# A decoder layer on one core: the first norm's last squares and root under the query product, keys and values leave PSUM unscaled, sums on VectorE, first loads in another order

## The chip, the core and the metric

The kernel runs on one core of a Trainium2 chip. The core has five engines that run side by side, each with its own in-order instruction stream: TensorE (PE, matrix products; PEld is its weight load), VectorE (DVE), ScalarE (ACT), GpSimd (POOL) and SyncE (SP, which here only issues transfers). Transfers between the chip's main memory and the on-chip memory SBUF are issued by SP, ACT or POOL and carried out by 16 DMA engines. TensorE writes to PSUM, from where DVE or ACT take the results. The metric is the device time of one execution in microseconds (us), and of several runs the median.

## The reference

One layer of a decoder for 320 tokens (256 of a prompt, 8 x 8 samples), D = 2048, all in float32. The beginning matters here:

```python
def rms_norm(x, g):
    xf = x.astype(jnp.float32)
    y = xf * lax.rsqrt(jnp.mean(xf * xf, axis=-1, keepdims=True) + EPS)
    return (y * g.astype(jnp.float32)).astype(x.dtype)
...
    xn = rms_norm(x, g_mix)
    z = xn @ w_in          # [B | C | h | q | k | v | gate_conv | gate_attn]
    u = c_gate * h_conv
    conv_out, conv_state = short_conv(u, conv_prev, w_conv)
    y_conv = (b_gate * conv_out) @ w_conv_out
    ...                    # banded attention of 16 query heads over 4 key/value heads
    merged = jax.nn.sigmoid(gate_c) * y_conv + jax.nn.sigmoid(gate_a) * y_attn
    h = x + merged @ w_o
    hn = rms_norm(h, g_ffn)
    h = h + (jax.nn.silu(hn @ w_gate) * (hn @ w_up)) @ w_down
```

The outputs are the final norm of h, and the new keys, values and convolution state. The scaled keys and values are outputs themselves.

## The kernel before

**Products.** Activations lie with features on the 128 partitions and the 320 tokens along the free side: x is 16 chunks of 128 x 320. A float32 product is made of three: each weight tile is split into a rounded part `whi` (an ACT copy, line 94) and a residual `wlo` (a DVE subtraction, line 95), and each x chunk into `xh_t` (ACT, line 244) and `xl_t` (DVE, line 245); TensorE adds whi.xh, whi.xl and wlo.xh. In the order of `passes` the wlo matmuls run a few steps behind the whi matmuls of the same tile. The raw weights have four buffers (`wraw`), the parts three each (`whi`, `wlo`): a load waits until DVE has read the raw buffer, a split until TensorE has read the part buffer.

**The norm is applied late.** x goes into the products unscaled (times g_mix only); the scale 1/root of each token, `rb`, is multiplied onto the results. `rb` needs the sum of squares of all 16 chunks (`xacc`): a square per chunk (even chunks on ACT, odd on DVE, lines 318 and 320), added up by POOL (line 322), one matmul with `ones` that sums over partitions (`prb`, line 350), and `rstd_of`/`inv_root` (lines 177 to 189): scale, ACT's root, DVE's reciprocal, three DVE products that refine it. `rbq` and `rbsq` follow from `rb`.

**The stages.** First the keys and values: `kv_product` makes all four 128-column groups of k and v at once, in nine weight tiles (two of one x chunk, seven of two; lines 265 to 293), into all four `acc` banks of PSUM. Ahead of it TensorE runs seven matmuls on a constant (`wm`, line 238). Inside it, at one place of each tile, `x_prep` makes the parts of the next two x chunks, and `tick()` lets `start_rest` issue the next piece of side work: squares and sums, the small loads on POOL's queue, the position-bias table (`pe_`, line 337, `e_sb`, `e_scr`, `bias_s`) and at last the root. After the product, kT and vT are the PSUM results times `rb` (lines 358 and 360). Then four query products (`in_pair`, named q, 16 weight tiles in all) with `kv_work` as side work: `kv_natural` transposes vT and kT on TensorE, `keys_twice` makes the keys' parts. The first query tile's split is tied behind the root by `first`. After q come the products C, H, B with the attention as side work, the gates, the output products and the feed-forward part; they are not touched.

**First loads.** x comes in eight blocks (`XB`, in chunks of 128 x 320: 1, 1, 2, 2, 2, 2, 2, 4). SP issues x blocks 0, 1, 2, then by turns a key/value weight tile and an x block; ACT issues the first two weight tiles. `small_loads` (POOL) waits for x chunk 3.

**Order.** A scheduler lays out each engine's stream from data dependences and the `after(...)` marks; pools of buffers (`bufs=`) add the waits.

Of the kernel before, what the change touches and what calls it, by code (L numbers as in the profile page):

```python
# [8 lines left out]
F32 = mybir.dt.float32  # L9
F32R = mybir.dt.float32r  # L10
AF = mybir.ActivationFunctionType
ALU = mybir.AluOpType
# [5 lines left out]
T = TP + NB * TS  # L18
DC = 1024
NH, NKV, HD, GRP = 16, 4, 64, 4  # L20
DKV = NKV * HD
WIN = 128
NBK = 32
FF = 5632
EPS = 1e-6
NEG = -1.0e30
P = 128
KC = D // P
CW = 256
KT = 4  # L30
O_B, O_C, O_H, O_Q = 0, DC, 2 * DC, 3 * DC
O_GC = O_Q + NH * HD
O_GA = O_GC + D
EL = 384
# [7 lines left out]
def hybrid_layer(ctx: ExitStack, tc: tile.TileContext, a: dict, o: list):  # L42
    nc = tc.nc
# [16 lines left out]
    def ps_aux(name):  # L60
        return aux.tile([P, 512], F32, tag="aux", name=name)
# [3 lines left out]
    def u(s):  # L65
        uid[0] += 1
        return f"{s}_{uid[0]}"

    def after(*marks):

        es = ExitStack()
        for m in marks:
            es.enter_context(tc.issue_after(m.ins))
        return es
# [3 lines left out]
    def tmp(tag, name):  # L78
        return wk.tile([P, UL], F32, tag=tag, name=u(name))
# [7 lines left out]
        lo = wp.tile([P, KT, CW], F32R, tag="wlo", name=u("wlo"), bufs=3)  # L87
        return hi, lo

    first = []  # L90

    def split_to(hi, lo, src):
        with after(*first):
            last["hi"] = nc.scalar.activation(hi, src, AF.Copy)  # L94
            last["lo"] = nc.vector.tensor_sub(lo, src, hi.bitcast(F32))  # L95

    def load_cols(w, k0, n, c0, behind=()):
        raw = raw_tile()
# [7 lines left out]
    side_work = [None]  # L106
# [67 lines left out]
    def rstd_of(ss, shape, name, pool, out=None):  # L174

        v = pool.tile(shape, F32, tag=f"rs_v{shape[1]}", name=u(name))
        nc.vector.tensor_scalar(v, ss, 1.0 / D, EPS, op0=ALU.mult, op1=ALU.add)
        return inv_root(v, shape, name, pool, out)
# [28 lines left out]
    def in_pair(c0, name, **kw):  # L207
        return product(lambda k0, n: load_cols(w_in, k0, n, c0), KC, xh, xl, name, **kw)
# [4 lines left out]
    kT = zz.tile([P, 2, T], F32, name="kT")  # L213
    vT = zz.tile([P, 2, T], F32, name="vT")
    vn = [zz.tile([P, DKV], F32, name=f"vn{t}") for t in range(3)]


    sp = ExitStack()
# [15 lines left out]
    )  # L234

    wm = ps_aux("wm")
    for _ in range(7):
        nc.tensor.matmul(wm, busy[:, :P], busy, start=True, stop=True)

    def x_prep(kc):  # L240
        if kc == 0:
# [10 lines left out]

    def load_kv(k0, n):
        raw = wp.tile([P, KT // 2, CK], F32, tag="wraw", name=u("wraw"), bufs=4)
        (nc.scalar if k0 < 2 else nc.sync).dma_start(raw[:, :n, :], w_kv[0, :, k0:k0 + n, :])
        hi = wp.tile([P, KT // 2, CK], F32R, tag="whi", name=u("whi"), bufs=3)
        lo = wp.tile([P, KT // 2, CK], F32R, tag="wlo", name=u("wlo"), bufs=3)
        with after(*mark[k0]):
            split_to(hi[:, :n, :], lo[:, :n, :], raw[:, :n, :])
        return hi, lo  # L260

    def kv_product(tiles, x_after):

        ps = [ps_acc(u("kv")) for _ in range(4)]
        k0 = 0
        x_prep(0)
        for i, n in enumerate(tiles):
            hi, lo = load_kv(k0, n)
            if i == 0:
                x_prep(1)  # L270
            for b in x_after.get(i, ()):
                x_load(b)
            order = [(k, c) for k in range(n) for c in range(4)]
            if k0 + n == KC:
                order.sort(key=lambda kc: kc[1])
            seq = passes(order, k0 + n == KC)
            if i == 0:
                seq.sort(key=lambda kcm: kcm[2])
            for k, c, m in seq:
                kc = k0 + k  # L280
                if k0 and (k, c, m) == (0, 1 if n == 1 or k0 + 2 * n == KC else 3, 0) and k0 + n < KC:
                    x_prep(k0 + n)
                    x_prep(k0 + n + 1)
                    tick()
                w, x = ((hi, xh), (hi, xl), (lo, xh))[m]
                last["mm"] = nc.tensor.matmul(  # L286
                    ps[c][:, :T], w[:, k, c * P:(c + 1) * P], x(kc),
                    start=(kc == 0 and m == 0), stop=(kc == KC - 1 and m == 2),
                )
            k0 += n  # L290
            if i == 0:
                tick()
        return ps

    rel = st.tile([NBK, NH], F32, name="rel")
    oh = st.tile([NBK, WIN], F32, name="oh")
    sk = a["sinks"]
    gate = st.tile([P, 1], F32, name="gate")

# [8 lines left out]
            nc.gpsimd.dma_start(st_sb, a["state_t"])  # L308
            nc.gpsimd.dma_start(blk, a["c_block"])

    xacc = st.tile([P, T], F32, name="xacc")

    def squares(*chunks):

        for k in chunks:
            t = xacc if k == 0 else st.tile([P, T], F32, tag="sq", name=u("sq"), bufs=4)
            if k % 2 == 0:
                nc.scalar.activation(t, hT[:, k, :], AF.Square)
            else:
                nc.vector.tensor_mul(t, hT[:, k, :], hT[:, k, :])  # L320
            if k:
                nc.gpsimd.tensor_tensor(xacc, xacc, t, op=ALU.add)

    def start_rest():
        squares(0)
        yield
        small_loads()
        squares(1)
        yield
        squares(2, 3, 4)  # L330
        yield
        squares(5, 6, 7)
        yield
        squares(8, 9, 10, 11)
        nc.vector.tensor_scalar(nsink, sink_bc, -1.0, None, op0=ALU.mult)
        pe_ = ps_aux("pe_")
        nc.tensor.matmul(pe_[:NH, :WIN], rel, oh, start=True, stop=True)
        e_sb = st.tile([NH, EL], F32, name="e_sb")
        nc.vector.memset(e_sb, NEG)
        nc.vector.tensor_copy(e_sb[:, WIN - 1:2 * WIN - 1], pe_[:NH, :WIN])  # L340
        nc.gpsimd.dma_start(e_scr, e_sb)
        yield
        squares(12, 13, 14, 15)
        yield
        nc.gpsimd.dma_start(
            bias_s, bass.AP(e_scr.tensor, e_scr.offset + WIN - TS, [[EL, NH], [1, TS], [1, WIN + TS]])
        )
        yield
        prb = ps_aux("prb")
        nc.tensor.matmul(prb[:, :T], ones, xacc, start=True, stop=True)  # L350
        rstd_of(prb[:, :T], [P, T], "r1", st, out=rb)

    side_work[0] = start_rest()
    ps_kv = kv_product([1, 1] + [2] * 7, {0: (2,), 2: (3,), 3: (4,), 4: (5, 6), 5: (7,)})
    for _ in side_work[0]:
        pass
    for c in range(2):
        nc.vector.tensor_mul(kT[:, c, :], ps_kv[c][:, :T], rb)
    for c in range(2):
        nc.vector.tensor_mul(vT[:, c, :], ps_kv[2 + c][:, :T], rb)  # L360
    nc.vector.tensor_scalar(rbq, rb, HD ** -0.5, None, op0=ALU.mult)
    nc.vector.tensor_mul(rbsq, rb, rb)
    sp.close()
    first += [last["root"], last["inv"]]

    yp = ExitStack()
    yy = yp.enter_context(tc.tile_pool(name="yy", bufs=1))
# [279 lines left out]
            yield  # L647

    def kv_work():
        for t in range(3):  # L650
            kv_natural(t)
            yield
        yield from keys_twice()
# [23 lines left out]
    side_work[0] = kv_work()  # L677
    for j in range(2):
        for gp in range(2):
            ps = in_pair(O_Q + (j * 2 + gp) * CW, "q", loaded=first.clear)  # L680
            pending.append(lambda j=j, gp=gp, ps=ps: q_out(j, gp, ps))
    side_work[0] = attention()

# [433 lines left out]
```

## Time and profile before

| what | value |
|---|---|
| median of 3 runs | 1690.41 us (1690.31 to 1691.01) |
| the profiled execution, its own time | 1690.07 us |
| its span, from first to last instruction | 1688.0 us |
| TensorE busy, share of the span | 1672.2 us, 99% |
| DVE / ACT / POOL busy | 902.4 / 645.9 / 97.3 us |
| mean granted TensorE clock | 0.997 |
| first matmul of keys and values, of the queries | 5.11 us, 44.53 us |

How to read the rows that follow. In a timeline a row has the start and the length in us, the engine, the line of the kernel, the operation, what it writes and reads (buffer numbers left out), the shape, and how many such instructions in a row were merged (x4); in brackets the idle time of the engine before it and what ended that. Rows of one engine can overlap a little, as a following instruction enters before the one ahead has left. In a row of waits: the total, the number of waits, the longest. In a table of stages: first the stretch (us from the span's start) and its length, then for each engine the busy time and in brackets the number of instructions, then the granted TensorE clock (1.00 is full), the busy share of the DMA engines and GB/s. A row of a load ends with the time from issue to landing.

### The profile page before, as it was taken

What the parts mean: (1) busy time and instruction counts of PE and PEld (TensorE: products, weight loads), DVE (VectorE), ACT (ScalarE), POOL (GpSimd) and SP (SyncE); (2) the same over time, 40 slices, a digit from 0 to 9 for tenths busy, and PEclk for the clock granted to TensorE, in tenths of its full rate; (3) what the DMA queues carried; (4) which work ended last, traced back from release to release, by engine and by line L of the source; (5) the groups of instructions that cost most, each with busy time, mean ns of one, the idle gap of its engine ahead of it and who ended that gap; (6) DMA issues with size and microseconds to landing.
All of it is one profiled execution on the core that took longest, in us unless ns stands there. A gap on an engine that the chain in (4) does not pass through costs nothing.

```text
span 1688.0 us, 26587 instructions
## 1 busy us (share of the span) xinstructions
PE 1672.2 (99%) x11016; PEld 1624.3 (96%) x11016; DVE 902.4 (53%) x1351; ACT 645.9 (38%) x898; POOL 97.3 (6%) x135
## 2 busy tenths in 40 slices
PE   8999999999999999999999999999999999999998
PEld 7999999999999999999999999998888999999887
DVE  8679564444444445546555555553444455555556
ACT  5455443333333333334333333333333333334344
POOL 6001311000000002320000000000000000000000
PEclk9999999999999999999999999999999999999999
DMA  6554545544454444444444444445555444444543
GB/s 229 162 156 143 183 134 164 176 149 149 150 150 150 150 150 150 150 149 148 150 150 150 150 150 150 150 150 151 150 151 150 150 150 150 150 150 150 174 145 105
DMA packets 76336, 258.13 MB, mean 153 GB/s; under 512 B 8440, under 2 KB 15016, under 8 KB 76088
## 3 DMA queue, kind: packets, MB, share of 16 engines
q1 hardware_dynamic: 73960, 250.01, 47.5%
q0 software_dynamic: 1968, 5.90, 1.2%
q8 instruction: 86, 1.41, 0.3%
q10 hardware_dynamic: 288, 0.52, 0.1%
q14 instruction: 34, 0.28, 0.0%
HBM read 253.29 MB, written 5.08 MB: 153 GB/s over the span
## 4 chain that ended last, share of the span: by engine, by line
PE 98%; POOL 1%; DVE 1%; DMA 0%; issue 0%; SPq 0%; ACT 0%; DVEq 0%; POOLq 0%
PE fg L141 18%; PE fu L141 18%; PE dn L837 9%; PE ga L141 7%; PE wo L141 7%; PE gc L141 7%; PE dn L845 6%; PE H L141 3%; PE C L141 3%; PE B L141 3%; PE q L141 3%; PE ya L141 3%; PE yc L141 3%; PE dl L841 2%; PE dr L992 1%; PE kv L286 1%
## 5 line engine op out<-in xcount | busy, mean ns | idle before, releaser
L95 DVE TENSOR_TENSOR wlo<-wraw,whi 128x1024 fp32r<-128x1024 f32 (+1 forms) x464 | 568.7, 1226 | 642.4 <-ACT whi L94 633.8
L94 ACT ACTIVATE whi<-wraw 128x1024 fp32r<-128x1024 f32 (+1 forms) x464 | 490.5, 1059 | 811.3 <-PE dn L837 179.9
L837 PE MATMUL dn<-a_t,whi 128*128 128x512 f32 x672 | 231.0, 396 | 0.0
L141 PE MATMUL fu<-hh_t,whi 128*128 128x320 f32 x704 | 212.6, 310 | 0.0
L141 PE MATMUL fg<-hh_t,whi 128*128 128x320 f32 x704 | 212.4, 309 | 0.0
L141 PE MATMUL fu<-hl_t,whi 128*128 128x320 f32 x704 | 212.3, 309 | 0.0
L141 PE MATMUL fg<-hl_t,whi 128*128 128x320 f32 x704 | 212.3, 309 | 0.0
L141 PE MATMUL fg<-hh_t,wlo 128*128 128x320 f32 x704 | 164.0, 309 | 0.0
L141 PE MATMUL fu<-hh_t,wlo 128*128 128x320 f32 x704 | 164.0, 309 | 0.0
L845 PE MATMUL dn<-a_t,wlo 128*128 128x320 f32 x672 | 159.5, 309 | 0.0
L837 PEld LDWEIGHTS dn<-a_t,whi 128*128 128x128 f32 x672 | 125.1, 188 | 24.6 <-issue 0.5
L141 PEld LDWEIGHTS fu<-hl_t,whi 128*128 128x128 f32 x704 | 132.2, 188 | 0.1
L141 PEld LDWEIGHTS fu<-hh_t,whi 128*128 128x128 f32 x704 | 132.1, 188 | 0.1
L141 PEld LDWEIGHTS fg<-hl_t,whi 128*128 128x128 f32 x704 | 132.2, 188 | 0.0
L141 PEld LDWEIGHTS fg<-hh_t,whi 128*128 128x128 f32 x704 | 132.1, 188 | 0.0
L845 PEld LDWEIGHTS dn<-a_t,wlo 128*128 128x128 f32 x672 | 118.0, 188 | 11.7
L141 PEld LDWEIGHTS fu<-hh_t,wlo 128*128 128x128 f32 x704 | 118.5, 188 | 0.0
L141 PEld LDWEIGHTS fg<-hh_t,wlo 128*128 128x128 f32 x704 | 118.5, 188 | 0.0
L141 PE MATMUL wo<-m_h,whi 128*128 128x320 f32 x256 | 77.2, 309 | 0.0
L141 PE MATMUL ga<-xh_t,whi 128*128 128x320 f32 x256 | 77.1, 308 | 0.0
L141 PE MATMUL ga<-xl_t,whi 128*128 128x320 f32 x256 | 77.1, 308 | 0.0
L141 PE MATMUL gc<-xh_t,whi 128*128 128x320 f32 x256 | 77.1, 308 | 0.0
(278 smaller groups left out, 2759.2 us busy)
## 6 DMA issues: line engine op xcount, KB each, us to landing
wraw<-in_w_in_dram SPq DMA_DIRECT2D x128, 512.0 KB, 3.8
wraw<-in_w_gate_dram SPq DMA_DIRECT2D x88, 512.0 KB, 3.8
wraw<-in_w_up_dram SPq DMA_DIRECT2D x88, 512.0 KB, 3.8
wraw<-in_w_down_dram SPq DMA_DIRECT2D x88, 512.0 KB, 3.6
wraw<-in_w_o_dram SPq DMA_DIRECT2D x32, 512.0 KB, 3.7
wraw<-in_w_conv_out_dram SPq DMA_DIRECT2D x16, 512.0 KB, 3.7
wraw<-in_w_attn_out_dram SPq DMA_DIRECT2D x16, 512.0 KB, 3.7
wraw<-in_w_kv_dram SPq DMA_DIRECT2D x7, 512.0 KB, 6.9
```

Source lines behind the costliest of these rows:

```text
L94: last["hi"] = nc.scalar.activation(hi, src, AF.Copy)
L95: last["lo"] = nc.vector.tensor_sub(lo, src, hi.bitcast(F32))
L141: last["mm"] = nc.tensor.matmul(ps[c][:, :T], w[:, k, c * P:(c + 1) * P], x(kc), start=(kc == 0 and i == 0), stop=(kc == nk - 1 and i == 2),)
L286: last["mm"] = nc.tensor.matmul(ps[c][:, :T], w[:, k, c * P:(c + 1) * P], x(kc), start=(kc == 0 and m == 0), stop=(kc == KC - 1 and m == 2),)
L837: nc.tensor.matmul(ps[c], parts[k][0][:, cs], a_t[:, k, 0:512], start=k == 0, stop=False)
L841: nc.tensor.matmul(low[:, :w], a_t[:, k, 512:], parts[k][0], start=k == 0, stop=k == nf - 1)
L845: last["mm"] = nc.tensor.matmul(ps[c][:, :T], parts[k][1][:, cs], a_t[:, k, 0:T], start=False, stop=k == nf - 1)
L992: last["mm"] = nc.tensor.matmul(ps[:, :CW], x, w, start=(t == 2 and k == 0 and m == 0), stop=(k == nf - 1 and m == len(ms) - 1),)
```

## The change

- POOL no longer adds squares. All squares are made on ACT, into buffers of the work pool (`tmp`, two for each of four tags), and all sums on DVE.
- The squares of chunks 12 to 15, the sum over partitions, the root, `rbq`, `rbsq` and the position-bias table move out of `start_rest` into `first_norm`, side work at the head of `kv_work`, under the query products. The two matmul groups `pe_` and `prb` stand behind the second query tile.
- ACT copies keys and values from PSUM unscaled; `first_norm` multiplies them by `rb` in SBUF later, and the transposes of `kv_natural` come three ticks later.
- The tie `first` of the query splits to the root is gone.
- The second weight tile is issued by SP, behind x block 1 and ahead of x block 2; x block 2 was issued ahead of the weight tiles. The first weight tile is copied by ACT in two halves. The warm-up is six matmuls of 512 columns and three of 128.
- `x_prep` and `tick` stand a little later in most tiles.

```diff
@@ -87,12 +87,9 @@
         lo = wp.tile([P, KT, CW], F32R, tag="wlo", name=u("wlo"), bufs=3)
         return hi, lo
 
-    first = []
-
     def split_to(hi, lo, src):
-        with after(*first):
-            last["hi"] = nc.scalar.activation(hi, src, AF.Copy)
-            last["lo"] = nc.vector.tensor_sub(lo, src, hi.bitcast(F32))
+        last["hi"] = nc.scalar.activation(hi, src, AF.Copy)
+        last["lo"] = nc.vector.tensor_sub(lo, src, hi.bitcast(F32))
 
     def load_cols(w, k0, n, c0, behind=()):
         raw = raw_tile()
@@ -213,6 +210,10 @@
     kT = zz.tile([P, 2, T], F32, name="kT")
     vT = zz.tile([P, 2, T], F32, name="vT")
     vn = [zz.tile([P, DKV], F32, name=f"vn{t}") for t in range(3)]
+    xacc = zz.tile([P, T], F32, name="xacc")
+    rel = zz.tile([NBK, NH], F32, name="rel")
+    oh = zz.tile([NBK, WIN], F32, name="oh")
+    e_sb = zz.tile([NH, EL], F32, name="e_sb")
 
 
     sp = ExitStack()
@@ -234,8 +235,8 @@
     )
 
     wm = ps_aux("wm")
-    for _ in range(7):
-        nc.tensor.matmul(wm, busy[:, :P], busy, start=True, stop=True)
+    for n in [512] * 6 + [P] * 3:
+        nc.tensor.matmul(wm[:, :n], busy[:, :P], busy[:, :n], start=True, stop=True)
 
     def x_prep(kc):
         if kc == 0:
@@ -252,11 +253,16 @@
 
     def load_kv(k0, n):
         raw = wp.tile([P, KT // 2, CK], F32, tag="wraw", name=u("wraw"), bufs=4)
-        (nc.scalar if k0 < 2 else nc.sync).dma_start(raw[:, :n, :], w_kv[0, :, k0:k0 + n, :])
+        (nc.scalar if k0 == 0 else nc.sync).dma_start(raw[:, :n, :], w_kv[0, :, k0:k0 + n, :])
         hi = wp.tile([P, KT // 2, CK], F32R, tag="whi", name=u("whi"), bufs=3)
         lo = wp.tile([P, KT // 2, CK], F32R, tag="wlo", name=u("wlo"), bufs=3)
         with after(*mark[k0]):
-            split_to(hi[:, :n, :], lo[:, :n, :], raw[:, :n, :])
+            if k0 == 0:
+                nc.scalar.activation(hi[:, 0, :CW], raw[:, 0, :CW], AF.Copy)
+                last["hi"] = nc.scalar.activation(hi[:, 0, CW:], raw[:, 0, CW:], AF.Copy)
+                last["lo"] = nc.vector.tensor_sub(lo[:, 0, :], raw[:, 0, :], hi[:, 0, :].bitcast(F32))
+            else:
+                split_to(hi[:, :n, :], lo[:, :n, :], raw[:, :n, :])
         return hi, lo
 
     def kv_product(tiles, x_after):
@@ -278,7 +284,7 @@
                 seq.sort(key=lambda kcm: kcm[2])
             for k, c, m in seq:
                 kc = k0 + k
-                if k0 and (k, c, m) == (0, 1 if n == 1 or k0 + 2 * n == KC else 3, 0) and k0 + n < KC:
+                if k0 and (k, c, m) == (0, 3 if n > 1 else 1, 0) and k0 + n < KC:
                     x_prep(k0 + n)
                     x_prep(k0 + n + 1)
                     tick()
@@ -292,8 +298,6 @@
                 tick()
         return ps
 
-    rel = st.tile([NBK, NH], F32, name="rel")
-    oh = st.tile([NBK, WIN], F32, name="oh")
     sk = a["sinks"]
     gate = st.tile([P, 1], F32, name="gate")
 
@@ -308,60 +312,61 @@
             nc.gpsimd.dma_start(st_sb, a["state_t"])
             nc.gpsimd.dma_start(blk, a["c_block"])
 
-    xacc = st.tile([P, T], F32, name="xacc")
-
     def squares(*chunks):
 
         for k in chunks:
-            t = xacc if k == 0 else st.tile([P, T], F32, tag="sq", name=u("sq"), bufs=4)
-            if k % 2 == 0:
-                nc.scalar.activation(t, hT[:, k, :], AF.Square)
-            else:
-                nc.vector.tensor_mul(t, hT[:, k, :], hT[:, k, :])
+            t = tmp("t" + "abcd"[k % 4], "sq")[:, :T] if k else xacc
+            nc.scalar.activation(t, hT[:, k, :], AF.Square)
             if k:
-                nc.gpsimd.tensor_tensor(xacc, xacc, t, op=ALU.add)
+                nc.vector.tensor_add(xacc, xacc, t)
 
     def start_rest():
         squares(0)
         yield
         small_loads()
         squares(1)
-        yield
-        squares(2, 3, 4)
-        yield
-        squares(5, 6, 7)
-        yield
-        squares(8, 9, 10, 11)
+        for k in range(2, 12, 2):
+            yield
+            squares(k, k + 1)
+
+    side_work[0] = start_rest()
+    ps_kv = kv_product([1, 1] + [2] * 7, {1: (2,), 2: (3,), 3: (4,), 4: (5, 6), 5: (7,)})
+    for _ in side_work[0]:
+        pass
+    for c in range(2):
+        nc.scalar.activation(kT[:, c, :], ps_kv[c][:, :T], AF.Copy)
+    for c in range(2):
+        nc.scalar.activation(vT[:, c, :], ps_kv[2 + c][:, :T], AF.Copy)
+    sp.close()
+
+    class spare:
+
+        @staticmethod
+        def tile(shape, dtype, tag, name):
+            return tmp({"v": "tb", "s": "tc", "r": "td"}[tag[3]], name)[:, :shape[1]]
+
+    def first_norm():
+
+        squares(12, 13, 14, 15)
         nc.vector.tensor_scalar(nsink, sink_bc, -1.0, None, op0=ALU.mult)
-        pe_ = ps_aux("pe_")
+        nc.vector.memset(e_sb, NEG)
+        yield
+        prb, pe_ = ps_aux("prb"), ps_aux("pe_")
         nc.tensor.matmul(pe_[:NH, :WIN], rel, oh, start=True, stop=True)
-        e_sb = st.tile([NH, EL], F32, name="e_sb")
-        nc.vector.memset(e_sb, NEG)
+        nc.tensor.matmul(prb[:, :T], ones, xacc, start=True, stop=True)
+        rstd_of(prb[:, :T], [P, T], "r1", spare, out=rb)
+        nc.vector.tensor_scalar(rbq, rb, HD ** -0.5, None, op0=ALU.mult)
+        for z in (vT, kT):
+            for c in range(2):
+                nc.vector.tensor_mul(z[:, c, :], z[:, c, :], rb)
+        nc.vector.tensor_mul(rbsq, rb, rb)
         nc.vector.tensor_copy(e_sb[:, WIN - 1:2 * WIN - 1], pe_[:NH, :WIN])
         nc.gpsimd.dma_start(e_scr, e_sb)
-        yield
-        squares(12, 13, 14, 15)
-        yield
         nc.gpsimd.dma_start(
             bias_s, bass.AP(e_scr.tensor, e_scr.offset + WIN - TS, [[EL, NH], [1, TS], [1, WIN + TS]])
         )
-        yield
-        prb = ps_aux("prb")
-        nc.tensor.matmul(prb[:, :T], ones, xacc, start=True, stop=True)
-        rstd_of(prb[:, :T], [P, T], "r1", st, out=rb)
-
-    side_work[0] = start_rest()
-    ps_kv = kv_product([1, 1] + [2] * 7, {0: (2,), 2: (3,), 3: (4,), 4: (5, 6), 5: (7,)})
-    for _ in side_work[0]:
-        pass
-    for c in range(2):
-        nc.vector.tensor_mul(kT[:, c, :], ps_kv[c][:, :T], rb)
-    for c in range(2):
-        nc.vector.tensor_mul(vT[:, c, :], ps_kv[2 + c][:, :T], rb)
-    nc.vector.tensor_scalar(rbq, rb, HD ** -0.5, None, op0=ALU.mult)
-    nc.vector.tensor_mul(rbsq, rb, rb)
-    sp.close()
-    first += [last["root"], last["inv"]]
+        for _ in range(3):
+            yield
 
     yp = ExitStack()
     yy = yp.enter_context(tc.tile_pool(name="yy", bufs=1))
@@ -647,6 +652,7 @@
             yield
 
     def kv_work():
+        yield from first_norm()
         for t in range(3):
             kv_natural(t)
             yield
@@ -677,7 +683,7 @@
     side_work[0] = kv_work()
     for j in range(2):
         for gp in range(2):
-            ps = in_pair(O_Q + (j * 2 + gp) * CW, "q", loaded=first.clear)
+            ps = in_pair(O_Q + (j * 2 + gp) * CW, "q")
             pending.append(lambda j=j, gp=gp, ps=ps: q_out(j, gp, ps))
     side_work[0] = attention()
```

More of the change, by code (lines that the diff above doesn't have):

```diff
@@ L328, in start_rest @@
         squares(1)
-        yield
-        squares(2, 3, 4)
-        yield
-        squares(5, 6, 7)
-        yield
-        squares(8, 9, 10, 11)
-        nc.vector.tensor_scalar(nsink, sink_bc, -1.0, None, op0=ALU.mult)
-        pe_ = ps_aux("pe_")
-        nc.tensor.matmul(pe_[:NH, :WIN], rel, oh, start=True, stop=True)
-        e_sb = st.tile([NH, EL], F32, name="e_sb")
-        nc.vector.memset(e_sb, NEG)
+        for k in range(2, 12, 2):
[16 more added lines that the diff above has]
+        squares(12, 13, 14, 15)
+        nc.vector.tensor_scalar(nsink, sink_bc, -1.0, None, op0=ALU.mult)
+        nc.vector.memset(e_sb, NEG)
+        yield
+        prb, pe_ = ps_aux("prb"), ps_aux("pe_")
+        nc.tensor.matmul(pe_[:NH, :WIN], rel, oh, start=True, stop=True)
+        nc.tensor.matmul(prb[:, :T], ones, xacc, start=True, stop=True)
[5 more added lines that the diff above has]
+        nc.vector.tensor_mul(rbsq, rb, rb)
         nc.vector.tensor_copy(e_sb[:, WIN - 1:2 * WIN - 1], pe_[:NH, :WIN])
         nc.gpsimd.dma_start(e_scr, e_sb)
-        yield
-        squares(12, 13, 14, 15)
-        yield
         nc.gpsimd.dma_start(
```

## The prediction

> **What bounds the kernel now.** I read the waits of TensorE over the whole execution first, then a table of busy time by stage, then the timeline of TensorE where the table shows holes, last VectorE (DVE), GpSimd (POOL) and ScalarE (ACT) at those places.
>
> ```profile
> span 1688.0 us, 26587 instructions
> PE kv L286 <- DVE wlo L95: 4.2, 3, 1.9
> PE kv L286 <- ACT whi L94: 2.5, 3, 1.9
> PE wm L238 <- DVE busy L160: 1.5, 1, 1.5
> ```
>
> These three are all the waits that TensorE has: 8.2 us of 1688, the first two inside the key/value product (line 286). From the first query matmul on it never waits, so what this change can bring or cost lies ahead of that matmul, or is a new wait put behind it.
>
> ```profile
> core 0: us, PE busy (x) PEld busy (x) DVE busy (x) ACT busy (x) POOL busy (x), PEclk, DMA share, GB/s
> 5.11:9.30 4.19, 3.99 (x25) 3.73 (x25) 3.32 (x8) 3.48 (x7) 1.45 (x4) 1.00 1.02 369
> 9.30:22.85 13.55, 12.92 (x82) 11.85 (x82) 13.53 (x16) 8.44 (x16) 11.65 (x14) 1.00 0.88 323
> 22.85:29.47 6.62, 3.09 (x20) 2.83 (x20) 4.89 (x8) 3.31 (x7) 6.38 (x5) 1.00 0.26 79
> 29.47:36.30 6.83, 4.94 (x19) 4.54 (x18) 6.83 (x6) 2.18 (x3) 6.22 (x8) 0.50 0.35 81
> 36.30:44.53 8.23, 8.23 (x56) 8.07 (x55) 7.38 (x10) 2.53 (x4) 0.00 (x0) 1.00 0.53 200
> ```
>
> From 9.30 to 22.85 DVE is busy without a hole and POOL nearly so; from 22.85 to 29.47 TensorE works less than half the time; for the next 6.83 us its granted clock is 0.50.
>
> ```profile
> 9.30 0.41 PE L286 MATMUL kv<-xh_t,whi 128*128 128x320 f32 x1 [0.19 <-ACT whi L94]
> 14.97 0.41 PE L286 MATMUL kv<-xh_t,wlo 128*128 128x320 f32 x1 [0.63 <-DVE wlo L95]
> 24.52 0.42 PE L286 MATMUL kv<-xh_t,wlo 128*128 128x320 f32 x1 [1.67 <-DVE wlo L95]
> 28.99 0.42 PE L286 MATMUL kv<-xh_t,whi 128*128 128x320 f32 x1 [1.86 <-ACT whi L94]
> 33.01 0.63 PE L286 MATMUL kv<-xh_t,wlo 128*128 128x320 f32 x1 [1.89 <-DVE wlo L95]
> 44.53 0.31 PE L141 MATMUL q<-xh_t,whi 128*128 128x320 f32 x1
> 56.37 45.76 PE q L141 x312
> ```
>
> The matmul at 9.30 opens the third of nine weight tiles (tiles 2 to 8 have 24 matmuls each), the one at 44.53 opens q. In the last row, from the chain of waits, 312 matmuls take 45.76 us: 0.1467 each, 3.52 a tile.
>
> Why the holes:
>
> ```profile
> 7.52 1.01 DVE L245 SCALAR_TENSOR_TENSOR xl_t<-xv,xh_t 128x320 fp32r<-128x320 f32 x2
> 8.45 0.48 DVE L320 TENSOR_TENSOR sq<-xv 128x320 f32<-128x320 f32 x1
> 9.28 1.23 DVE L95 TENSOR_TENSOR wlo<-wraw,whi 128x1024 fp32r<-128x1024 f32 x1 [0.35 <-ACT whi L94]
> 10.42 2.27 DVE L245 SCALAR_TENSOR_TENSOR xl_t<-xv,xh_t 128x320 fp32r<-128x320 f32 x2
> 11.40 2.02 POOL L322 TENSOR_TENSOR xacc<-xacc,sq 128x320 f32<-128x320 f32 x2
> 12.61 1.17 DVE L320 TENSOR_TENSOR sq<-xv 128x320 f32<-128x320 f32 x1
> 19.02 10.38 POOL L322 TENSOR_TENSOR xacc<-xacc,sq 128x320 f32<-128x320 f32 x7
> 26.16 0.47 ACT L318 ACTIVATE sq<-xv 128x320 f32<-128x320 f32 x1 [4.37 <-POOL xacc L322]
> ```
>
> POOL's sums start at 11.40. Before them two residuals (line 245) take 1.01 us on DVE, beside them 2.27; a square 0.48, then 1.17. POOL takes 1.5 us a sum (10.38 for 7). Squares wait for POOL to release their four buffers (4.37 us at 26.16), and weight splits queue behind squares on ACT and DVE. So POOL paces the stage twice: through buffers and by slowing DVE.
>
> **The change part by part.** (1) The sums leave POOL, 12 of the 15 for DVE in this stage (chunks 0 to 11), all squares go to ACT; the last four squares and sums, the root and its three products move behind the first q tiles. Per tile of 3.52 us on TensorE, DVE then has a split 1.23, two residuals 1.01 and two sums. The trace has no such sum on DVE; the nearest rows are the square, 0.48 alone and 1.17 beside POOL. I take 0.48, since POOL sums nothing now: 1.23 + 1.01 + 0.96 = 3.20, below 3.52. The third tile's split can begin at 9.28 as it did and is due 8 matmuls into the tile, 9.30 + 1.17 = 10.47; it ends at 10.5, and from there DVE gains 0.32 us a tile.
>
> ```profile
> 8.18 1.06 ACT L94 ACTIVATE whi<-wraw 128x1024 fp32r<-128x1024 f32 x1 [0.39 <-DMA wraw<-in_w_kv_dram]
> 9.15 1.00 ACT L244 ACTIVATE xh_t<-xv 128x320 fp32r<-128x320 f32 x2
> 10.05 0.45 ACT L318 ACTIVATE sq<-xv 128x320 f32<-128x320 f32 x1
> ```
>
> ACT has 1.06 + 1.00 + 2 x 0.45 = 2.96 a tile, also below 3.52. The added squares cost nothing under that cover.
>
> (2) Loads. The slow weight tile is the sixth (issued at 7.63):
>
> ```profile
> wraw<-in_w_kv_dram SPq DMA_DIRECT2D x1, 512.0 KB, 10.2
> 13.50:16.00 2.50, 1.87 (x13) 1.61 (x12) 2.50 (x4) 1.44 (x4) 2.00 (x2) 1.00 0.60 167
> 2.13 0.43 SPq L255 DMA_DIRECT2D wraw<-in_w_kv_dram  x1
> ```
>
> It lands at 17.83, after a spell at 167 GB/s; with its copy (1.06) it is ready at 18.9. Without holes TensorE wants it at 9.30 + 3 x 3.52 = 19.86: covered by 0.97 us; the later tiles are issued as DVE frees their buffers, now earlier. Reordering puts the second weight tile on SyncE's queue ahead of x block 2, so that block and the third weight tile are issued one step (0.43) later, while the bytes ahead of them stay the same. Bounds for the third tile's start: +0.43, or -0.36 (9.30 against 8.94, where the second tile's last matmul gives way). I take 0. The first tile's ACT copy in two halves and the finer warm-up may start TensorE up to 0.48 us earlier (its wait there), but the third tile starts with its load, so nothing is gained by that.
>
> [...]
>
> (3) The key/value stage. Third tile to q now: 44.53 - 9.30 = 35.23. Without holes: 168 x 0.1467 = 24.64. Difference 10.59: idle 0.63 + 1.67 + 1.86 + 1.89 = 6.05; half clock 4.94 / 2 = 2.47; two foreign matmul groups 0.93 (next fence); the rest, 1.1, is restarting after four holes. The foreign groups are not saved, they run under q:
>
> ```profile
> 18.39 0.39 PE L337 MATMUL pe__304<-oh,rel 32*16 32x128 f32 x2
> 37.41 0.54 PE prb L350 x2
> ```
>
> Gain 10.59 - 0.93 = 9.66.
>
> The clock falls 0.5 us after the second long hole has ended and nowhere else in the stage, so I count it as caused by the holes. [...]
>
> (4) Under q. New on TensorE's in-order stream: the two groups behind q tile 1, then transposes of vT behind q tile 4, which need the scaled vT.
>
> ```profile
> 37.98 0.49 DVE L177 TENSOR_SCALAR r<-prb 128x320 f32<-128x320 f32 x1 [0.21 <-PE prb L350]
> 38.51 0.47 ACT L184 ACTIVATE r<-r 128x320 f32<-128x320 f32 x1 [6.86 <-DVE r L177]
> 39.01 2.15 DVE L185 RECIPROCAL r<-r 128x320 f32<-128x320 f32 x1 [0.54 <-ACT r L184]
> 42.25 0.49 DVE L189 SCALAR_TENSOR_TENSOR rb<-r,r 128x320 f32<-128x320 f32 x1
> 44.60 0.88 DVE L360 TENSOR_TENSOR vT<-kv,rb 128x320 f32<-128x320 f32 x2
> 45.39 0.32 DVE L361 TENSOR_SCALAR rbq<-rb 128x320 f32<-128x320 f32 x1
> ```
>
> q starts at 9.30 + 24.64 = 33.94; its tile 1 ends at 40.98, the groups at 41.91. On DVE the split of q tile 4 stands ahead of the norm and needs the buffers that tile 1 frees at 40.98: copy 1.06, split 1.23, so 43.3. Then 0.5, root 0.5, reciprocal 2.2: 46.5. The split of tile 5 (buffers free at 45.43) ends at 47.7; three products of about 0.5, rbq 0.32, vT 0.88: 50.4. The transposes stand at 41.91 + 3 x 3.52 = 52.47. Margin 2.0 us, so no wait. Behind vT on DVE come kT (0.88 like vT), rbsq and the query outputs, then the split of tile 6, due at 41.91 + 4 x 3.52 + 1.17 = 57.2. The query outputs run in this stage in the kernel before too, and TensorE waits for nothing there (first fence). The four ACT copies out of PSUM (0.45 each, the square's row; a copy from PSUM is not in the trace) fall to ACT's free time: in 57 us of q it was busy 26 ("44.53:102.00" below).
>
> ```profile
> 44.53:102.00 57.47, 57.47 (x397) 57.41 (x396) 36.46 (x63) 25.91 (x39) 2.31 (x4) 1.00 0.53 166
> ```
>
> Sum against the execution's own time: 1690.07 (span 1688.0 and 2.07 around it) - 9.66 = 1680.41. It lies 0.34 under the median of the runs, so the median should read 1680.75; I say 1680.8.
>
> **Rivals.** B: one hole stays. For it: the sixth tile's cover is only 0.97 us and DVE's gain only 0.32 a tile; against: all of POOL's sums are gone. Price, a hole as large as the largest, 1.89 + 0.27 of restart, and the half clock with it, 2.47: 4.6, so 1685.4; a small hole alone, 0.5 to 1.2, gives 1681.3 to 1682.
>
> [...]
>
> D, slower: DVE becomes the bound. If its slow instances are not POOL's doing but that of DMA or ACT traffic, a tile costs 1.23 + 2.27 + 2 x 1.17 = 5.84, 2.32 above TensorE's, over seven tiles 16.2: 1680.8 + 16.2 = 1697.0. It decides from 3.52 + 9.66 / 7 = 4.90 us a tile on. Against: the fast pair at 7.52 ran at the DMA share 1.02.
>
> E: the gain moves under q, the change only shifts the wait: the scaled vT would have to come 2.0 us late before it costs, 11.7 late to cost everything (1690.4). For it: TensorE is in order and the norm waits twice for other engines; against: each wait is counted above.
>
> **How the numbers follow.** Forecast with its small variants (1679.4 to 1682): 0.70. B with a large hole 0.13, C 0.08, D 0.04, E 0.05, half of it between 1682 and 1687. The low end takes the early start (0.36) and the two foreign groups for nothing (0.93): 1679.5; the high end reaches B: 1685.2. Below and above lie about 0.15. This kernel's measurement tells 0.2%, 3.4 us, from no change: faster by more 0.94, within 0.02, slower 0.04.
>
> **What would show it.** Right: TensorE waits in the key/value product add to under 1 us, the granted clock reads 1.00 from about 6 us on, q's first matmul starts at about 34, residual pairs on DVE take 1.0 throughout, no wait at the vT transposes. Wrong: a hole at the sixth tile (B), 0.50 in the clock column without holes (C), DVE over 3.5 us a tile (D), a wait of TensorE on vT or on the sum of squares (E).

## The result, and the profile after

| | before | after |
|---|---|---|
| median of 6 runs each | 1690.15 us (1689.46 to 1691.01) | 1681.49 us (1680.61 to 1681.77) |
| the profiled execution, its own time | 1690.07 us | 1681.54 us |
| its span | 1688.0 us | 1679.6 us |
| first matmul of the third weight tile | 9.30 us | 10.41 us |
| first matmul of q | 44.53 us | 35.05 us |

The ratio of the times is 0.9948, with a 95% interval of 0.9935 to 0.9961: faster by about half a per cent. The forecast was 1680.8 us.

One point in the list of changes is smaller than it reads: by the condition in the diff, `x_prep` and `tick` stand later in one weight tile alone, the eighth (`k0` = 12).

All waits of TensorE in the changed kernel (total, number, longest):

```profile
PE wm L239 <- DVE busy L157: 1.5, 1, 1.5
PE kv L292 <- ACT whi L261: 0.6, 1, 0.6
```

The waits for weight splits are gone; what is left lies ahead of the first weight tile. The same stages as in the forecast's table:

```profile
5.11:9.30 4.19, 4.19 (x17) 4.19 (x18) 3.55 (x7) 3.57 (x8) 0.85 (x3) 1.00 0.94 362
9.30:22.85 13.55, 13.55 (x94) 13.55 (x93) 12.96 (x24) 13.53 (x28) 2.60 (x5) 1.00 0.93 354
22.85:29.47 6.62, 6.62 (x47) 6.62 (x46) 5.49 (x8) 3.75 (x6) 0.00 (x0) 1.00 0.65 199
29.47:36.30 6.83, 6.83 (x49) 6.83 (x48) 4.05 (x9) 4.38 (x8) 0.00 (x0) 1.00 0.68 223
```

From 9.30 on TensorE (first column) is busy throughout, and where the clock stood at 0.50 it reads 1.00. ACT is busy for 13.53 of 13.55 us and yet nothing waits for it: at the forecast's 2.96 us a tile that is 4.6 tiles of work, while TensorE's 94 matmuls are 3.9 tiles. It works ahead, and is down to 3.75 of 6.62 in the next stretch. The first row is the one that is worse: 17 matmuls where the kernel before had 25.

Single instructions of the changed kernel, from its timelines:

```profile
1.46 3.06 PE L239 MATMUL wm<-busy 128*128 128x512 bf16 x9 [1.46 <-DVE busy L157]
5.11 1.44 PE L292 MATMUL kv<-xh_t,whi 128*128 128x320 f32 x4 [0.59 <-ACT whi L261]
6.35 1.27 PE L292 MATMUL kv<-xl_t,whi 128*128 128x320 f32 x4
2.60 0.43 SPq L256 DMA_DIRECT2D wraw<-in_w_kv_dram  x1
8.69 1.06 ACT L91 ACTIVATE whi<-wraw 128x1024 fp32r<-128x1024 f32 x1 [0.31 <-DMA wraw<-in_w_kv_dram]
10.41 0.31 PE L292 MATMUL kv<-xh_t,whi 128*128 128x320 f32 x1
10.93 1.01 DVE L246 SCALAR_TENSOR_TENSOR xl_t<-xv,xh_t 128x320 fp32r<-128x320 f32 x2
14.91 0.48 DVE L321 TENSOR_TENSOR xacc<-xacc,sq 128x320 f32<-128x320 f32 x1
35.05 0.31 PE L138 MATMUL q<-xh_t,whi 128*128 128x320 f32 x1
42.51 0.81 PE L356 MATMUL prb<-xacc,ones 128*128 128x320 f32 x2
50.39 0.89 DVE L361 TENSOR_TENSOR vT<-vT,rb 128x320 f32<-128x320 f32 x2
53.72 0.38 PE L394 MATMUL pk<-ident,vT 128*128 128x128 f32 x2
```

The time came out of the stretch from the third tile to q: 35.05 - 10.41 = 24.64 us, to the second decimal the 168 x 0.1467 of the forecast. A little of it was lost ahead of that stretch. The third tile starts 1.11 us later than before. Its load is issued at 2.60 in place of 2.13, and takes 6.1 us to land in place of 6.0; its ACT copy starts at 8.69 in place of 8.18 (0.51 later), and released by it alone the tile could have opened at about 9.8 (the copy takes 1.06). But TensorE had not finished the first two tiles by then: their matmuls ran at about half rate for long (four of them take 1.27 us at 6.35, and 0.75 at 6.01 in the kernel before). One microsecond of the changed kernel, then the same one of the kernel before:

```profile
6.00:7.00 1.00, 1.00 (x6) 1.00 (x5) 0.82 (x3) 1.00 (x3) 0.00 (x0) 1.00 1.02 378
```

```profile
6.00:7.00 1.00, 1.00 (x9) 1.00 (x8) 0.64 (x2) 1.00 (x3) 0.00 (x0) 1.00 0.87 347
```

Six matmuls against nine with TensorE busy all the time. (The clock column says 1.00 in both; ahead of the throttle's first record it tells nothing, and the count does.) The throttle's first record of full rate stands at 5.58 us before and at 8.81 after. In this profile, then, the load order accounts for half a microsecond and the cold clock for another 0.6. Which of these belongs to the change was not plain from one profile.

### The profile page after: what moved, and what is told of

It is laid out like the page before. It is cut to its first block, busy times and chain, and to the rows that moved or that the text cites. A ratio compares the mean times of both kernels' runs of the same rounds, so it can differ in the third digit from the quotient of the medians.

```text
span 1679.6 us, 26587 instructions
## 1 busy us (share of the span) xinstructions
PE 1669.9 (99%) x11018; PEld 1624.0 (97%) x11018; DVE 895.7 (53%) x1358; ACT 650.9 (39%) x911; POOL 78.3 (5%) x120
## 4 chain that ended last, share of the span: by engine, by line
PE 99%; DMA 0%; DVE 0%; ACT 0%; DVEq 0%; issue 0%
PE fg L138 18%; PE fu L138 18%; PE dn L843 9%; PE ga L138 7%; PE wo L138 7%; PE gc L138 7%; PE dn L851 6%; PE C L138 3%; PE H L138 3%; PE B L138 3%; PE q L138 3%; PE ya L138 3%; PE yc L138 3%; PE dl L847 2%; PE kv L292 2%; PE dr L998 1%
## 5 line engine op out<-in xcount | busy, mean ns | idle before, releaser
L138 PE MATMUL wo<-m_l,whi 128*128 128x320 f32 x256 | 77.1, 309 | 0.0
```

What stands on the lines that cost most here:

```text
L138: last["mm"] = nc.tensor.matmul(ps[c][:, :T], w[:, k, c * P:(c + 1) * P], x(kc), start=(kc == 0 and i == 0), stop=(kc == nk - 1 and i == 2),)
```

## The experiments

Two things had to be tested: that POOL's sums were what set the pace of the key/value stage (the forecast's mechanism, against the half clock and the move of the norm), and what the lost microsecond ahead of the third tile is (theory "order": the new order of loads; theory "warm-up": the lighter warm-up heats the clock later; theory "window": the clock heats at a moment that differs from run to run, whatever the warm-up). The kernel before had a median of 1691.03 us beside the first four, 1691.19 beside the next four and 1690.79 beside the last three.

**1. The changed kernel again**, nothing edited.

> The changed kernel once more. In its first profile TensorE's clock was at full rate from 8.85 us on (before the change from 5.57 us), the first matmul of keys and values stood at 5.11 us in both, and the third weight tile began at 10.41 us in place of 9.30. [...] Theory 'warm-up': the new warm-up with its 0.59 us of idle sets it, so again 8.85 and 10.4. Time 1681.5 by both, within 0.5.

Measured: 1681.46 us (1680.92 to 1683.52), ratio 0.9945 (0.9932 to 0.9957). Timelines of this run:

```profile
4.91 1.05 PE L292 MATMUL kv<-xh_t,whi 128*128 128x320 f32 x4 [0.39 <-ACT whi L261]
8.95 1.06 ACT L91 ACTIVATE whi<-wraw 128x1024 fp32r<-128x1024 f32 x1 [0.20 <-DMA wraw<-in_w_kv_dram]
10.05 0.42 PE L292 MATMUL kv<-xh_t,whi 128*128 128x320 f32 x1 [1.16 <-ACT whi L91]
```

The same program, and now full rate from 5.35 us: the first four matmuls take 1.05 us in place of 1.44. The third tile still opens at 10.05, after waiting 1.16 us for its load. The cold clock was that one profile's; the late load is there in both.

**2. The old warm-up.**

```diff
-    for n in [512] * 6 + [P] * 3:
+    for n in [512] * 7:
```

> The changed kernel with the old warm-up, seven matmuls of 512 columns. Theory 'warm-up': full rate from about 5.5 us, third tile at about 9.8 us (then its load decides), time 0.6 us less than the changed kernel's, 1680.9. Theory 'window': no fixed difference from the changed kernel; full rate anywhere between 5.4 and 8.9, 1681.5 within 0.5.

Measured: 1681.2 us (1680.93 to 1681.35), ratio 0.9941 (0.9929 to 0.9954); full rate from 5.98 us, later than the lighter warm-up of experiment 1 had it.

**3. A longer warm-up**, which leaves no gap ahead of the first tile.

```diff
-    for n in [512] * 6 + [P] * 3:
+    for n in [512] * 7 + [P] * 6:
```

> The changed kernel with a longer warm-up, seven matmuls of 512 columns and six of 128, which ends at about 5.1 us, so that TensorE is not idle ahead of the first product. Theory 'warm-up': full rate by 5.5 us, third tile at 9.8, 1680.9. [...]

Measured: 1681.48 us (1680.8 to 1681.66), ratio 0.9942 (0.993 to 0.9955); full rate from 6.51 us. The third tiles of experiments 2 and 3, one row from each timeline:

```profile
9.58 0.41 PE L292 MATMUL kv<-xh_t,whi 128*128 128x320 f32 x1 [0.38 <-ACT whi L91]
```

```profile
10.07 0.41 PE L292 MATMUL kv<-xh_t,whi 128*128 128x320 f32 x1 [0.61 <-ACT whi L91]
```

The longer warm-up of experiment 3 made neither the clock nor the tile earlier than in experiment 1. In experiment 2 the tile opened earlier (9.58 against 10.05), but its clock was later; it was the load that came earlier (copy at 8.46 against 8.95). All three tiles wait for that load. So "warm-up", as the fixed cause of the lost microsecond, falls.

**4. The old order of the first loads.**

```diff
-        (nc.scalar if k0 == 0 else nc.sync).dma_start(raw[:, :n, :], w_kv[0, :, k0:k0 + n, :])
+        (nc.scalar if k0 < 2 else nc.sync).dma_start(raw[:, :n, :], w_kv[0, :, k0:k0 + n, :])
...
-    ps_kv = kv_product([1, 1] + [2] * 7, {1: (2,), 2: (3,), 3: (4,), 4: (5, 6), 5: (7,)})
+    ps_kv = kv_product([1, 1] + [2] * 7, {0: (2,), 2: (3,), 3: (4,), 4: (5, 6), 5: (7,)})
```

> The changed kernel with the loads in the old order (second weight tile from ACT's queue, x block 2 ahead of the weight tiles of SP). Theory 'order costs': the ACT copy of the third tile starts at about 8.2 us in place of 8.69; the third tile begins at 9.3 us if the clock is at full rate by 5.6, else still at about 10.4, as tiles 1 and 2 at half rate last until then; time 0 to 0.5 us less than the changed kernel's. Theory 'order helps': the copy starts no earlier than 8.69, the second tile is later, and the time is 0 to 0.5 us more.

Measured: 1680.81 us (1680.57 to 1681.92), ratio 0.9942 (0.9928 to 0.9956). Its timelines:

```profile
8.25 1.06 ACT L91 ACTIVATE whi<-wraw 128x1024 fp32r<-128x1024 f32 x1 [0.17 <-DMA wraw<-in_w_kv_dram]
9.36 0.41 PE L292 MATMUL kv<-xh_t,whi 128*128 128x320 f32 x1 [0.47 <-ACT whi L91]
```

The copy is back near the 8.18 of the kernel before, the third tile at 9.36.

**5. The kernel before, with its holes filled.** Seven matmuls on the constant, whose result nothing reads, ahead of each of the three long holes, so that the clock should not fall.

```diff
+                if c == 0 and k == 0 and (i, m) in ((5, 2), (6, 0), (6, 2)):
+                    fill = ps_aux("fill")
+                    for _ in range(7):
+                        nc.tensor.matmul(fill, busy[:, :P], busy, start=True, stop=True)
```

> The kernel before, with seven extra matmuls of 512 constant columns (about 1.5 us) put into TensorE's stream ahead of each of the three longest holes of the key/value stage; they compute nothing that is used. Theory 'holes cool the clock': the granted clock stays at 1.00 through the stage, the half clock's price (2.47 us) goes, the time falls by 1.5 to 2.5 us against the kernel before, to about 1688. [...]

Measured: 1689.63 us (1689.23 to 1690.74), ratio 0.9992 (0.9983 to 1.0002): no difference that can be told from none. Two stages, then the waits for splits:

```profile
22.85:29.47 6.62, 5.73 (x33) 3.93 (x32) 6.62 (x7) 5.27 (x9) 6.27 (x6) 1.00 0.28 85
29.47:36.30 6.83, 5.09 (x32) 3.90 (x31) 6.83 (x7) 0.33 (x1) 4.91 (x6) 1.00 0.48 95
```

```profile
PE kv L290 <- DVE wlo L95: 3.1, 3, 1.7
PE kv L290 <- ACT whi L94: 0.8, 2, 0.5
```

The clock stays at 1.00 in the stage. The other executions agree: the mean clock is 0.999 in nine of the ten filled ones, and 0.995 to 0.998 in the 17 of the kernel before beside them. So the holes had caused the half clock (0.50 without holes was the sign of rival C). What the half clock cost is less plain. In the profiles q begins at 43.95, only 0.58 earlier than before: DVE is busy throughout both stretches, and TensorE at full rate still waits for it. The medians lie 1.56 us apart, inside the 1.5 to 2.5 that I expected, but the interval of the ratio includes no difference at all and reaches down to 0.9983, a gain of 2.9 us. The 35 executions of the kernel before that stand beside the three rounds of experiments point the same way: on average 1690.2 us where the mean clock was 0.998 (8 of them), and 1691.8 where it was 0.995 (4). The three groups of fillers also take 1.69 us each. So this is no clean price of the half clock: somewhere between nothing and 2.9 us.

**6. The kernel before, with only the sums moved to DVE.**

```diff
-                nc.gpsimd.tensor_tensor(xacc, xacc, t, op=ALU.add)
+                nc.vector.tensor_add(xacc, xacc, t)
```

> The kernel before with only the sums moved from POOL to DVE; squares on ACT and DVE by turns, the norm in the key/value stage, keys and values scaled on the way out of PSUM. Theory 'POOL paces the stage': residual pairs back at 1.0 us on DVE, the holes of 1.7 to 1.9 us gone or under 1 us, no half clock, q at 36 to 38 us in place of 44.5: 1682 to 1684. Rival D (slow DVE instances not POOL's doing): pairs stay at 2.2, holes grow by the sums, 1690 to 1697.

Measured: 1684.22 us (1683.41 to 1685.51), ratio 0.9962 (0.9947 to 0.9977). Timelines of DVE and of TensorE:

```profile
10.62 1.01 DVE L245 SCALAR_TENSOR_TENSOR xl_t<-xv,xh_t 128x320 fp32r<-128x320 f32 x2
23.64 0.41 PE L286 MATMUL kv<-xh_t,wlo 128*128 128x320 f32 x1 [1.71 <-DVE wlo L95]
37.91 0.38 PE L141 MATMUL q<-xh_t,whi 128*128 128x320 f32 x1 [0.41 <-DVE kT L358]
```

One line brings 7.0 of the 1691.19 us. The pair of residuals takes 1.01 where POOL's sums had made it 2.27; one long hole is left, and q waits 0.41 for the scaled kT. DVE still makes half of the squares here; with one more 0.48 on the forecast's 3.20 it would have 3.68 us of work a tile, an estimate from its rows, above TensorE's 3.52. Against the changed kernel's 1681.5 or so some 2.7 us are missing: squares on ACT, the move under q, the copies out of PSUM and the load order together, of which experiments 4 and 8 to 11 measure only a part.

**7. The changed kernel, with sums back on POOL**, squares by turns on ACT and DVE, four buffers; the norm stays under q.

```diff
-            t = tmp("t" + "abcd"[k % 4], "sq")[:, :T] if k else xacc
-            nc.scalar.activation(t, hT[:, k, :], AF.Square)
+            t = tmp("t" + "ab"[k % 2], "sq")[:, :T] if k else xacc
+            if k % 2 == 0:
+                nc.scalar.activation(t, hT[:, k, :], AF.Square)
+            else:
+                nc.vector.tensor_mul(t, hT[:, k, :], hT[:, k, :])
             if k:
-                nc.vector.tensor_add(xacc, xacc, t)
+                nc.gpsimd.tensor_tensor(xacc, xacc, t, op=ALU.add)
```

> The changed kernel with the sums back on POOL and the squares by turns on ACT and DVE in four buffers, as before the change; the last four squares and the root stay under q. Theory 'POOL paces the stage': pairs beside POOL's sums at 2.2 us again, squares wait for POOL, holes of 1 to 2 us in tiles 5 to 7: q at 38 to 42, 1685 to 1689. Rival 'the move under q brings the gain': no holes over 0.5 us, 1681 to 1682.5.

Measured: 1686.07 us (1685.71 to 1686.29), ratio 0.9971 (0.996 to 0.9982). Timelines:

```profile
14.03 2.81 POOL L324 TENSOR_TENSOR xacc<-xacc,sq 128x320 f32<-128x320 f32 x2 [0.49 <-DVE sq L322]
18.65 2.26 DVE L246 SCALAR_TENSOR_TENSOR xl_t<-xv,xh_t 128x320 fp32r<-128x320 f32 x2
24.73 0.41 PE L292 MATMUL kv<-xh_t,wlo 128*128 128x320 f32 x1 [2.16 <-DVE wlo L92]
```

With POOL's sums the pair of residuals takes 2.26 again, a hole of 2.16 us is back, and with it the half clock (0.50 from 25.45 to 28.86). About half of the gain is gone. Half of the squares went back to DVE with the sums, and what they alone add to the hole was not run; the slow pairs cannot come from them, as experiment 6 has the same squares on DVE and pairs of 1.01. Experiments 6 and 7 show from both sides that the sums on POOL set the pace.

**8. The changed kernel, with the last squares and the root back in the key/value stage**, `first_norm` taken apart; keys and values still leave PSUM unscaled.

```diff
+    def norm_rest():
+        yield from start_rest()
+        yield
...
-    side_work[0] = start_rest()
+    side_work[0] = norm_rest()
...
-        yield from first_norm()
```

> The changed kernel with the last four squares, the sum over partitions and the root issued in the key/value stage again (sums on DVE, keys and values still leave PSUM unscaled); the transposes come right after q tile 0. Theory 'the move hides a wait': TensorE waits for the sum of squares inside the key/value product and for the scaled vT at the first transposes, 1 to 4 us in all, 1682.5 to 1685.5. Rival 'the move is worth nothing once the sums are on DVE': no wait over 0.5 us, 1681.5 within 0.7.

Measured: 1682.24 us (1681.3 to 1682.59), ratio 0.9949 (0.9934 to 0.9963). TensorE's timeline at the third tile and where it waits:

```profile
9.49 0.41 PE L292 MATMUL kv<-xh_t,whi 128*128 128x320 f32 x1
31.17 0.81 PE L349 MATMUL prb<-xacc,ones 128*128 128x320 f32 x2 [0.62 <-DVE xacc L321]
```

The median is 0.75 us above the changed kernel's 1681.49, but that was taken beside a kernel before with a median of 1690.15 in place of 1691.19; the ratios, 0.9949 here and 0.9945 to 0.9948 for the changed kernel, cannot be told apart. So the medians decide for neither theory. Counted from the third tile to the end of the span (1680.4 - 9.49 = 1670.91, against 1669.17 to 1669.39 in the table below) it is 1.5 to 1.7 us; 0.62 of that is the wait for the sum of squares. The rest is short pauses in TensorE's stream, each under 0.25 us; what causes them stays open.

**9 to 11. The load order once more**, side by side: the changed kernel; the edit of experiment 4; the edits of 2 and 4 together.

Of the changed kernel:

> The changed kernel a third time, as the measure for the two beside it. Theory 'order costs': the ACT copy of the third key/value weight tile starts at 8.3 to 9.0 us from the span's start, as in the six profiles with the new load order so far, the third tile opens at 9.5 to 10.4, and the median is about 1681.4. Theory 'chance': the copy starts anywhere from 8.0 to 9.0 and the median lies within 0.3 us of the two versions beside it.

Of the old load order:

> The changed kernel with the old order of the first loads alone (second weight tile on ACT's queue, x block 2 ahead of the third weight tile), a second time. Theory 'order costs': copy of the third tile at 8.0 to 8.3, as in the four profiles with the old order, and a median 0.4 to 0.8 us below the changed kernel beside it, about 1680.8. Theory 'chance': copy anywhere from 8.0 to 9.0, median within 0.3 us of it.

Of the old load order and the old warm-up:

> The old load order and a warm-up of seven matmuls of 512 columns together, the version that should be at least as good as any so far. [...] Theory 'warm-up': full rate by 6 us every time and a median 0.3 us or more below the old order alone.

Measured: 1681.09 us (1680.68 to 1683.32), 1680.82 (1680.65 to 1681.0) and 1680.77 (1680.29 to 1680.92), with ratios of 0.9945 (0.9931 to 0.9958), 0.9941 (0.9928 to 0.9953) and 0.994 (0.9928 to 0.9952). Copy and third tile, one fence for each:

```profile
9.01 1.06 ACT L91 ACTIVATE whi<-wraw 128x1024 fp32r<-128x1024 f32 x1 [0.28 <-DMA wraw<-in_w_kv_dram]
10.11 0.41 PE L292 MATMUL kv<-xh_t,whi 128*128 128x320 f32 x1 [1.41 <-ACT whi L91]
```

```profile
8.14 1.06 ACT L91 ACTIVATE whi<-wraw 128x1024 fp32r<-128x1024 f32 x1
9.25 0.41 PE L292 MATMUL kv<-xh_t,whi 128*128 128x320 f32 x1 [0.42 <-ACT whi L91]
```

```profile
8.24 1.06 ACT L91 ACTIVATE whi<-wraw 128x1024 fp32r<-128x1024 f32 x1 [0.29 <-DMA wraw<-in_w_kv_dram]
9.63 0.31 PE L292 MATMUL kv<-xh_t,whi 128*128 128x320 f32 x1
```

The median of 9 lies only 0.27 us above that of 10, less than "order costs" asked for; these medians alone do not settle it, though all four with the new order in experiments 1 to 3 and 9 (1681.09 to 1681.48) lie above all three with the old one (1680.77 to 1680.82). The copies settle it. Over all profiles, the kernel before and its variants included, the new order has the copy at 8.36 to 9.01 us (seven profiles, mean 8.69), the old one at 7.99 to 8.25 (six, mean 8.15): 0.54 us, without overlap. In run 11 the clock was cold until 7.15 (in run 9 it was hot from 4.35), and the third tile came as the second one ended.

The profiles whose key/value stage is that of the changed kernel, put together (times in us):

| profile | load order | full rate from | third tile opens | span | span less third tile |
|---|---|---|---|---|---|
| after | new | 8.81 | 10.41 | 1679.6 | 1669.19 |
| 1, again | new | 5.35 | 10.05 | 1679.4 | 1669.35 |
| 2, old warm-up | new | 5.98 | 9.58 | 1678.9 | 1669.32 |
| 3, longer warm-up | new | 6.51 | 10.07 | 1679.4 | 1669.33 |
| 9, again | new | 4.35 | 10.11 | 1679.5 | 1669.39 |
| 4, old order | old | 4.80 | 9.36 | 1678.7 | 1669.34 |
| 10, old order | old | 4.95 | 9.25 | 1678.6 | 1669.35 |
| 11, order and warm-up | old | 7.15 | 9.63 | 1678.8 | 1669.17 |

The last column is the same to 0.22 us: what differs among these profiles is the moment at which the third tile opens, and next to nothing behind it. Of all kernels the eleventh has the lowest median, but it cannot be told from the changed kernel.

## Why the prediction was right, point by point

- **Sums and holes: right.** DVE's rows are the ones forecast, 1.01 for a pair of residuals and 0.48 for a single sum; no hole is left in the product, the sixth tile's included (rival B). Experiment 6 moves the sums alone off POOL, experiment 7 puts them back (with half of the squares on DVE), and the slow residuals, the holes and the time go with them. One reading was too simple: beside a sum a pair does not always take 2.27. The pair at 24.40 in the kernel before took 1.00 beside one (last section). DVE did not become the bound (rival D).
- **"Gain 10.59 - 0.93 = 9.66": right.** From the third tile to the end of the span it was 1688.0 - 9.30 = 1678.70 before and is 1669.19: a gain of 9.51. The stretch to q is 24.64 as forecast (24.83 in the profiles whose third tile waits for its load); behind it, from q's first matmul on, the span is 1.08 longer (1644.55 against 1643.47), where 0.93 was set down for the two foreign groups.
- **The parts of the 10.59: not shown to be savings of their own.** The sum holds since it is a difference of two whole stretches. That 2.47 of it was "half clock" is a way of counting: experiment 5 took the half clock away and brought 0.58 us in its profile and 1.56 by the medians, with an interval from nothing to 2.9.
- **Clock (rival C, "0.50 in the clock column without holes"): fell.** The stage without holes reads 1.00, and the filled kernel before does too.
- **Under q (rival E): fell.** vT is ready at 50.39 + 0.89 = 51.3 us (forecast 50.4, with q itself 1.1 later), its transposes stand at 53.72 (forecast 52.47): a margin of 2.4 us and no wait. The move is worth 1.5 to 1.7 us by the profile of experiment 8, while its medians do not tell it from nothing: either is far less than the sums.
- **"Bounds for the third tile's start: +0.43, or -0.36 ... I take 0": the term that was mis-sized.** It measured +1.11 in the profile. About 0.5 is the new load order, a little over the upper bound of that step (+0.43) and not its middle: the block and the weight tile are issued one step later, and land as much later. The other 0.6 is the clock, cold until 8.81, for which the forecast had no term; it is that profile's own, as experiments 1 and 9 run the same program hot from 5.35 and 4.35. Their third tiles open at 10.05 and 10.11 all the same, as the load came later there (copies at 8.95 and 9.01): +0.75 and +0.81, with no part of the clock in it. The forecast's sign "1.00 from about 6 us on" failed for the same reason: full rate came at 8.81 here, at 6.51 in experiment 3 and at 7.15 in experiment 11.
- **The sum.** 9.51 - 1.11 = 8.40 of span (1688.0 - 1679.6), and the own time fell by 8.53; the median is 0.7 us above the forecast. Where the forecast said that the first tile's copy in halves gains nothing, it was right: in the other seven profiles of the table the first matmul stands at 4.79 to 5.09 us in place of 5.11, and in six of them the third tile still waits for its load.

## What to carry to other kernels

Where one stage waits on several things, price it as a whole stretch, from the last instruction that the change does not touch to the first one behind it; its parts (holes, slow clock, restarts) need not be savings on their own. An engine that only adds up numbers off to the side can still set the pace, by holding buffers (a square waited 4.37 us for one here) and by holding up a neighbour (a pair of residuals took up to 2.27 us in place of 1.01), so look at how long the same instruction takes with and without it beside. At the beginning of a kernel, where TensorE waits for loads, a load issued one step later can cost that step (0.47 us of issue became 0.54 here); compare the start of the instruction that consumes the load over several profiles, since the spread of the medians can hide half a microsecond.

## What of the hardware was not expected

**The clock fell with no gap over 2.16 us.** In the kernel before it read 0.50 for 6.83 us, from 29.47 on, and in experiment 7 for 3.41 us, from 25.45 on; TensorE's longest gap in that stage was 1.89 us in the one and 2.16 us in the other. TensorE's busy time in the two stretches ahead of the fall, in the kernel before:

```profile
22.64:26.05 3.41, 1.74 (x12) 1.53 (x11) 2.75 (x6) 0.00 (x0) 3.41 (x1) 1.00 0.16 31
26.05:29.47 3.42, 1.56 (x11) 1.30 (x10) 2.35 (x3) 3.31 (x7) 3.19 (x5) 1.00 0.34 123
```

then in experiment 7 (the stretch ahead of the fall and the one at 0.50), and in experiment 6, whose clock did not fall:

```profile
22.03:25.45 3.42, 1.26 (x9) 1.00 (x8) 3.42 (x4) 3.42 (x7) 1.70 (x3) 1.00 0.07 26
25.45:28.86 3.41, 3.41 (x15) 3.41 (x15) 3.41 (x5) 1.52 (x2) 1.82 (x2) 0.50 0.50 154
```

```profile
20.68:24.09 3.41, 1.70 (x12) 1.44 (x11) 3.41 (x9) 3.41 (x7) 0.51 (x1) 1.00 0.29 113
24.09:27.51 3.42, 3.42 (x24) 3.28 (x23) 3.42 (x7) 1.30 (x2) 2.00 (x3) 1.00 0.73 196
```

In the stretch ahead of a fall TensorE was busy for 1.56 us (kernel before) and 1.26 us (experiment 7). After a stretch of the same length with 1.74 us (kernel before) or 1.70 us (experiment 6) the clock still read 1.00. Experiment 6 has one hole of 1.71 us, the kernel before three of 1.67 to 1.89. In experiment 5, with the holes filled but for gaps of up to 1.74 us, the clock stayed at 1.00; what it is about them that brings it down, how long they are or how close together, was not shown.

**The start of full rate is scattered**: 4.35 to 8.81 us over the 13 profiles, although the warm-up starts at 1.46 in all of them. The changed kernel alone, the same program each time, has it at 8.81, 5.35 and 4.35 (the profile after, experiments 1 and 9). What sets the moment was not shown.

**POOL and DVE hold each other up.** Residual pairs take 1.01 us without POOL's sums and up to 2.27 beside them, though the two engines share no data there. In the kernel before one sum of POOL's took 3.69 us, where two had taken 2.02 at 11.40, while DVE's instructions ran through it without a pause in their usual times:

```profile
22.45 3.69 POOL L322 TENSOR_TENSOR xacc<-xacc,sq 128x320 f32<-128x320 f32 x1
23.27 1.20 DVE L95 TENSOR_TENSOR wlo<-wraw,whi 128x1024 fp32r<-128x1024 f32 x1
24.40 1.00 DVE L245 SCALAR_TENSOR_TENSOR xl_t<-xv,xh_t 128x320 fp32r<-128x320 f32 x2
```

The sum ends at 26.14, 0.74 us behind the last of them. The other way round, a DVE product of only 16 columns took 0.84 us beside a sum in the kernel before, and 0.17 without sums in experiment 6:

```profile
21.56 0.84 DVE L335 TENSOR_SCALAR nsink<-sink_bc 128x16 f32<-128x16 f32 x1
```

```profile
20.96 0.17 DVE L335 TENSOR_SCALAR nsink<-sink_bc 128x16 f32<-128x16 f32 x1
```

So, by these rows, a sum on POOL cost a DVE instruction nothing (the split at 23.27, the pair at 24.40) or 0.67 us (0.84 in place of 0.17); what decides between the two was not shown. One thing more stays open: the pair at 10.42 that the forecast read starts 0.98 us ahead of the first recorded sum, so its first half is not explained; the pair at 18.65 in experiment 7 starts 0.91 us inside a row of sums (17.74 to 20.56) and ends 0.35 us behind it.
